# Wider rows for the two "xt" buffers, and another bank ring for the accumulators of the compressed keys and values

## The chip, the cores and the metric

The kernel runs on one core of one Trainium2 chip. The metric is the time of one execution in device microseconds; lower is better. Inputs and outputs are fp32.

## The reference

One layer of a hybrid decoder trunk (DEPTH is 1) on 512 tokens of 1024 features. The input is normalised, multiplied by one wide matrix, and the columns of the product are shared out among four token mixers: A (forgetting attention), B (a gated linear recurrence), C (sparse attention with compressed, selected and windowed keys) and D (chunked spatial gating). Each mixer's output is multiplied by its own SiLU gate and projected; the four are merged by sigmoid gates, projected once more and added to the input.

```python
xn = rms_norm(x, norm_g)
z = xn @ w_in
(qa, ka, va, fa, ga, xb, gb, qc, kcc, vcc, ksc, vsc, kwc, vwc, gate_c, gc,
 ud, vd, gd, mg) = jnp.split(z, split_at, axis=-1)
y_a = fox_attention(rms_norm(qa), rms_norm(ka), va, fa + b_forget)
y_b = rg_lru(xb, ...)
y_c = nsa_attention(rms_norm(qc), kcc, vcc, ksc, vsc, kwc, vwc, sigmoid(gate_c), ...)
y_d = spatial_gating(ud, vd, ...)
ys = stack([y_a * silu(ga), y_b * silu(gb), y_c * silu(gc), y_d * silu(gd)])
proj = einsum('bsnw,nwd->bsnd', ys, w_branch)
merged = sum(sigmoid(mg) * proj, axis=2)
return x + merged @ w_out
```

Inside `nsa_attention` the keys and values of overlapping blocks of 32 positions (stride 16) are compressed by a small network of two layers; the first layer is the part that the change touches:

```python
def compress(t, w1, w2):
    tb = t[:, blk_idx] + cmp_pos[None, None, :, None, :]
    tb = tb.transpose(0, 1, 3, 2, 4).reshape(B, n_cmp, G, CMP_BLOCK * dh)
    return jax.nn.silu(tb @ w1) @ w2
k_c = rms_norm(compress(k_cmp, wk1, wk2), kn_g)
v_c = compress(v_cmp, wv1, wv2)
```

## The kernel before

**Products.** Every fp32 product is made from three matmuls in a reduced fp32 format: both operands are split into a high and a low part, and high times high, high times low and low times high are added up in PSUM. A weight tile of 128 x 1024 (`load`, a 512-KB transfer by SyncE's queue into one of four raw buffers, names `r_...`) is cast to its high part by ScalarE or GpSimd and subtracted by VectorE to its low part (in two halves, names `w_...`). A projected block z is 128 x 512: eight slices of the contraction times three, so 24 matmuls of 512 columns each, in one PSUM bank.

**Stages.** First the input is loaded transposed. `x_norm` needs the row norms, which take time to arrive, so the first three projections (`ka`, `qa`, `va`, with the forget gates `z_gates`) are made from uh and ul, the parts of x times the norm's gain without the row norm; their results are scaled by row afterwards. In the natural layout (`nat`) uh and ul are the stationary operand and the weights move. `z_gates` has the small matrix gw as its stationary operand, and `rps` (the row norms spread over the partitions) the tile `ones`. Behind that all projections use the normed xh and xl. Then come A's attention, the projections and attention of C, laid between the projections of A's gate (`z_ga`), D's gate (`z_gd`), D's u (`z_ud`), C's gate and B; then the merge with its larger weights, which stand in shared sums that transfers with addition prepare in device memory (`dmg...`, `dwb...`), and the output.

**Order.** A planner (class `Order`) takes the instructions as the program emits them, with a cost for each, and writes one order for each of the five engines' queues; a queue is run strictly in that order. Which buffer a tile gets, and so which earlier reader it waits for, also enters the plan. The same emission with another bank can give another order on every queue.

**SBUF places.** Pools lay tiles out by size, one behind another, at the same place of every partition. The pool `xin` holds, in this sequence, the two buffers of the tag "xt" (`head0`/`head1`, later the `xt` tiles of `x_stats`, L415 and L659) and behind them ones, xr, uh, ul, neg, ssa, tsa, rb and gw.

**PSUM banks.** A bank holds 512 fp32 values for each partition. In this stage banks 0 and 1 are a ring of two for scores (`sbank`), 5, 6 and 7 a ring of three for projections (`zbank`). Banks are given out in turn as tiles are asked for. `hidden(nm)` (L1167) runs the first layer of the compression for keys (`hpsk`) and for values (`hpsv`): two halves of w1, and 16 matmuls of 256 columns into one bank, laid between the projections by `yield`. Then ScalarE and VectorE add the parts up (`hsk`, `hsv`), a transpose on TensorE (`tb<-identf,hsv`) and a SiLU follow (`hTv`, `hhv`), and `out` makes the second layer in an s bank (`cok`, `cov`). `sgd` is the reader of a `z_gd` bank: a ScalarE and then a VectorE operation.

Of the kernel before, what the change touches and what calls it, by code (L numbers as in the profile page):

```python
# [11 lines left out]
F32 = mybir.dt.float32  # L12
# [6 lines left out]
P = 128  # L19
S = 512  # L20
D = 1024
KD = D // P
# [41 lines left out]
def f32(ap):  # L64
    return ap.bitcast(F32)
# [260 lines left out]
def tile_hybrid_layer(ctx: ExitStack, tc: tile.TileContext, first, x, xT, units, small, bsp, out):  # L326
    nc = tc.nc
    order = Order(nc)
    ACT, DVE, POOL, PE, DMA = (_Engine(order, e) for e in ("ACT", "DVE", "POOL", "PE", "SP"))

    def pool(name, stack=ctx, **kw):
        return order.pool(stack.enter_context(tc.tile_pool(name=name, bufs=1, reuse_waits="tile", **kw)), stack,
                          kw.get("space"))
# [29 lines left out]
    def zbank(name):  # L363
        return ps_["z"].tile([P, S], F32, tag="z", bufs=ps_["nz"], name=name)
# [9 lines left out]
    def sbank(name):  # L374
        return ps_["s"].tile([P, S], F32, tag="s", bufs=2, name=name)

    def thalf():

        i = ps_["ti"] = (ps_["ti"] + 1) % (2 * len(ps_["tb"]))
        nt = len(ps_["tb"])  # L380
        return ps_["tb"][i % nt][:, 256 * (i // nt):256 * (i // nt) + 256]
# [12 lines left out]
    xin = pool("xin", early)  # L394
# [17 lines left out]
    order.on = True  # L412
    region = ExitStack()
    region.enter_context(tc.manual_schedule())
    head = [xin.tile([P, KD + D], F32, tag="xt", bufs=2, name=f"head{k}") for k in range(2)]  # L415
    for k in range(2):
        DMA.dma_start(head[k], first[:, k])
    maskm = cp.tile([P, S], F32, name="maskm")
    ones = xin.tile([P, P], F32R, name="ones")
    POOL.memset(f32(ones), 1.0)  # L420
# [16 lines left out]
    def hi_cast(dst, src):  # L437
        cnt["hi"] += 1
        if cnt["act"] and cnt["hi"] % cnt["act"] == 0:
            ACT.copy(dst, src)  # L440
        else:
            last["pool"] = POOL.tensor_scalar(dst, src, 1.0, 0.0, op0=ALU.mult, op1=ALU.add)

    def load(key, h):
        raw = wp.tile([P, 1024], F32, tag="raw", bufs=4, name=f"r_{key}{h}")
        DMA.dma_start(raw, units[UIDX[key], :, h * 1024:(h + 1) * 1024])
        return raw
# [149 lines left out]
    def rsqrt(v, y, t):  # L597

        I32 = mybir.dt.int32
        DVE.tensor_scalar(t.bitcast(I32), v.bitcast(I32), 1, None, op0=ALU.logical_shift_right)  # L600
        DVE.tensor_scalar(y.bitcast(I32), t.bitcast(I32), -1.0, float(0x5F3759DF), op0=ALU.mult, op1=ALU.add)
        for _ in range(3):
            DVE.tensor_tensor(t, y, y, op=ALU.mult)
            DVE.scalar_tensor_tensor(t, t, -0.5, v, op0=ALU.mult, op1=ALU.mult)
            DVE.scalar_tensor_tensor(y, t, 1.5, y, op0=ALU.add, op1=ALU.mult)
# [50 lines left out]
    def x_stats():  # L656
        st = cp.tile([P, 3, 4], F32, name="st")
        for t in range(4):
            xt = xin.tile([P, KD + D], F32, tag="xt", bufs=2, name=f"xt{t}")[:, 0:D]  # L659
            DMA.dma_start(xt, x[t * P:(t + 1) * P, :])  # L660
            ACT.activation(xt, xt, AF.Square, accum_out=st[:, 0, t:t + 1])
        DVE.tensor_scalar(st[:, 1, :], st[:, 0, :], 1.0 / D, EPS, op0=ALU.mult, op1=ALU.add)
        rsqrt(st[:, 1, :], rstd[:, 0, :], st[:, 2, :])
        DVE.tensor_tensor(rstd[:, 1, :], rstd[:, 0, :], rstd[:, 0, :], op=ALU.mult)
        DVE.tensor_scalar(rstd[:, 1, :], rstd[:, 1, :], 1.0 / 64, None, op0=ALU.mult)
# [78 lines left out]

    run(nat("ka", uh, ul, emit_z(zk_a, ssa, 0, 8, xin), fetch_first))
    x_stats()
    gq = nat("qa", uh, ul, emit_z(zq_a, ssa, 8, 8, xin))
    run(gq, 10)
# [383 lines left out]
    def mid(name):  # L1132
        return md.tile([P, 2, 1024], F32R, tag="mid", bufs=1, name=name)
# [13 lines left out]
    def compress():  # L1147
# [19 lines left out]
        def hidden(nm):  # L1167
            hps = None
            for h in range(2):
                raw = load("w1" + nm, h)  # L1170
                w = mid(f"w_w1{nm}{h}")
                hi_cast(w[:, 0, :], raw)
                DVE.tensor_tensor(w[:, 1, :], raw, f32(w[:, 0, :]), op=ALU.subtract)
                for _ in range(4):
                    yield 0.0
                if h == 0:
                    hps = zbank("hps" + nm)[:, 0:256]
                for k in range(8):
                    c = 8 * h + k
                    PE.matmul(hps.rearrange("p (j f) -> p j f", j=2), lhsT=ops[nm][:, c].rearrange("p j f -> p (j f)"),  # L1180
                              rhs=w[:, :, k * P:(k + 1) * P], start=c == 0, stop=c == 15)
                    if c < 15:
                        yield 0.15
            hs_ = ap.tile([P, S], F32, tag="ft", bufs=3, name="hs" + nm)
            POOL.memset(hs_[64:128, 0:P], 0.0)
            hs = hs_[0:64, 0:256]
            ACT.copy(hs, hps[64:128, :])
            DVE.tensor_tensor(hs, hps[0:64, :], hs, op=ALU.add)
            DVE.tensor_tensor(hs[:, 0:P], hs[:, 0:P], hs[:, P:2 * P], op=ALU.add)
            yield 0.15  # L1190
            yield 0.15
            hps = thalf()[:, 0:P]
            PE.transpose(hps, hs_[:, 0:P], identf)
            hps = hps[:, 0:64]
            hT = rp2.tile([P, 64], F32, tag="hT", bufs=2, name="hT" + nm)
            hh = rp2.tile([P, 2, 64], F32R, tag="hh", bufs=2, name="hh" + nm)
            ACT.activation(hT, hps, AF.Tanh, scale=0.5)
            DVE.scalar_tensor_tensor(hT, hT, 1.0, hps, op0=ALU.add, op1=ALU.mult)
            ACT.activation(hh[:, 0, :], hT, AF.Identity, scale=0.5)
            DVE.scalar_tensor_tensor(hh[:, 1, :], hT, 0.5, f32(hh[:, 0, :]), op0=ALU.mult, op1=ALU.subtract)  # L1200
            ops[nm] = hh
            yield 0.15
# [13 lines left out]
        for _ in range(4):  # L1216
            yield 0.0
        gk = hidden("k")
        for _ in range(8):
            yield next(gk)  # L1220
        y["c"], ug["t"] = tile8("y_c"), tile8("ug")
        yield from gk
        gv = hidden("v")
        for _ in range(4):
            yield next(gv)
# [781 lines left out]
```

## Time and profile before

| what | value |
|---|---|
| median of 3 runs | 687.35 us (687.24 to 687.45) |
| the profiled execution, its own time | 688.12 us |
| its span (first to last instruction) | 686.4 us |
| granted TensorE clock, mean | 0.999 |
| bytes moved by DMA | 145.45 MB, 212 GB/s |
| VectorE busy | 545.9 us of the span, 80% |
| ScalarE busy | 409.7 us, 60% |
| GpSimd busy | 196.5 us, 29% |

The profile is of one execution: the span is what its rows add up to, and the own time, 1.7 us more, is what that execution took by the measure of the runs. PE is TensorE's matmuls, PEld its loads of stationary operands, DVE is VectorE, ACT ScalarE, POOL GpSimd, SP SyncE. A row of the timeline gives start, length, engine, line, operation, output and inputs, tile sizes, and in brackets how long the engine was idle before and what released it. In a matmul's row the moving operand stands first and the stationary one last. A matmul's record is longer than the distance from one start to the next, because consecutive ones overlap; so a pace is read from starts. Where helpers emit an operation, its line is theirs (L290, L302), and tiles tell rows apart.

### The profile page before, as it was taken

How to read it: one execution, taken by the hardware profiler on the slowest of the kernel's cores; microseconds unless marked ns; L12 is line 12 of the kernel's file. 1: busy time of each engine (PE TensorE's matmuls, PEld its weight loads, DVE VectorE, ACT ScalarE, POOL GpSimd, SP SyncE). 2: the span in 40 equal slices, each digit the busy share in tenths (PEclk: the TensorE clock that was granted, in tenths of full speed). 3: DMA queues.
4: the chain of work that ended last, by engine and by line, in shares of the span. 5: the costliest groups of instructions: out<-in, count | busy, mean ns of one | idle time of the engine just before them, and what ended most of it. 6: DMA issues, size and time to landing. Idle time of an engine off the chain costs nothing.

```text
span 686.4 us, 9750 instructions
## 1 busy us (share of the span) xinstructions
PE 679.4 (99%) x3264; PEld 561.2 (82%) x3264; DVE 545.9 (80%) x1097; ACT 409.7 (60%) x772; POOL 196.5 (29%) x268
## 2 busy tenths in 40 slices
PE   9999999999999999999999999999999999999997
PEld 7888788888888877888887878888888888888886
DVE  6778778788578658889998697957889788848995
ACT  4554458476163247777666895555666666664961
POOL 4111674544346224544351221000202401300000
PEclk9999999999999999999999999999999999999999
DMA  8637076899979998965112224687999999896422
GB/s 322 253 121 245 32 197 211 236 211 262 248 230 302 250 305 214 246 172 106 62 32 71 84 93 169 193 313 241 253 338 300 345 318 368 250 339 207 149 94 93
DMA packets 35010, 145.45 MB, mean 212 GB/s; under 512 B 4096, under 2 KB 7552, under 8 KB 31744
## 3 DMA queue, kind: packets, MB, share of 16 engines
q1 hardware_dynamic: 30064, 108.78, 44.9%
q0 software_dynamic: 4608, 35.65, 24.2%
q8 instruction: 26, 0.43, 0.2%
q10 hardware_dynamic: 288, 0.39, 0.2%
q14 instruction: 24, 0.20, 0.1%
HBM read 139.57 MB, written 58.20 MB: 288 GB/s over the span
## 4 chain that ended last, share of the span: by engine, by line
PE 88%; ACT 4%; DMA 2%; DVE 2%; POOL 1%; issue 1%; DVEq 0%; SPq 0%; POOLq 0%; ACTq 0%
PE tb L290 4%; PE z_ka L290 3%; PE pj L302 3%; PE z_va L290 3%; PE z_qc L290 3%; PE z_qa L290 3%; PE z_xb L290 3%; PE z_ga L290 3%; PE z_vd L290 3%; PE z_gb L302 3%; PE z_kv L290 3%; PE o_s L290 3%; DMA dwb1s<-in_units_dram 2%; PE outy L302 2%; PE mg3y L302 2%; PE mg1y L302 2%
## 5 line engine op out<-in xcount | busy, mean ns | idle before, releaser
L302 POOL TENSOR_SCALAR mark<-mark 128x1 f32<-128x1 f32 x16 | 17.9, 1118 | 104.0 <-ACT mark L302 103.9
L302 DVE TENSOR_TENSOR w_mg<-r_mg,w_mg 128x512 fp32r<-128x512 f32 x48 | 31.8, 687 | 12.7 <-ACT w_mg L302 12.6
L302 PE MATMUL pj<-w_wb,yh 128*128 128x512 f32 x128 | 40.4, 389 | 0.0
L302 ACT CAST w_mg<-r_mg 128x1024 fp32r<-128x1024 f32 x24 | 25.2, 1050 | 11.8 <-issue 6.2
L302 PEld LDWEIGHTS pj<-w_wb,yh 128*128 128x128 f32 x128 | 24.0, 188 | 4.9
L290 POOL TENSOR_SCALAR p_s<-p_s,nm_s 128x512 f32<-128x512 f32 (+3 forms) x32 | 21.3, 681 | 22.4 <-DVE nm_s L290 18.7
L290 POOL TENSOR_SCALAR p_w<-p_w,nm_w 128x128 f32<-128x128 f32 (+3 forms) x32 | 18.4, 589 | 30.6 <-DVE nm_w L290 30.6
L290 ACT ACTIVATE p_s<-p_s,nm_s 128x512 f32<-128x512 f32 (+3 forms) x32 | 17.9, 561 | 13.7 <-DVE nm_s L290 13.2
L290 POOL TENSOR_SCALAR p_a<-p_a,nm_a 128x128 f32<-128x128 f32 (+3 forms) x32 | 20.9, 666 | 16.8 <-DVE nm_a L290 16.7
L290 ACT ACTIVATE p_w<-p_w,nm_w 128x256 f32<-128x256 f32 (+3 forms) x32 | 17.9, 561 | 12.5 <-DVE nm_w L290 12.4
L302 PE MATMUL pj<-w_wb,yl 128*128 128x512 f32 x64 | 25.2, 394 | 0.1
L290 PE MATMUL z_xb<-xh,w_xb 128*128 128x512 f32 x64 | 24.6, 410 | 0.0
L290 ACT CAST ph_a<-tb 128x512 fp32r<-128x512 f32 (+1 forms) x24 | 12.4, 517 | 18.8 <-PE tb L290 18.5
L290 PE MATMUL z_ud<-xh,w_ud 128*128 128x512 f32 x64 | 23.5, 405 | 0.0
L290 PE MATMUL z_gd<-xh,w_gd 128*128 128x512 f32 x64 | 22.5, 396 | 0.3 <-DVE sgd L290 0.3
L290 PE MATMUL z_ga<-xh,w_ga 128*128 128x512 f32 x64 | 21.9, 396 | 0.0
L302 PE MATMUL z_gb<-xh,w_gb 128*128 128x512 f32 x64 | 21.1, 396 | 0.0
L302 DVE TENSOR_TENSOR w_wb<-r_wb,w_wb 128x512 fp32r<-128x512 f32 x28 | 19.4, 717 | 1.4 <-POOL w_wb L302 0.9
L290 ACT ACTIVATE p_a<-p_a,nm_a 128x512 f32<-128x512 f32 (+3 forms) x32 | 17.8, 560 | 3.0 <-DVE nm_a L290 2.9
L290 DVE CUSTOM_DVE_ANT_0 p_a<-s_a,maskm 128x512 f32<-128x512 f32 (+3 forms) x32 | 15.0, 488 | 4.6 <-PE tb L290 2.8
L302 POOL TENSOR_SCALAR w_wb<-r_wb 128x1024 fp32r<-128x1024 f32 x8 | 10.8, 1350 | 26.9 <-PE pj L302 7.7
L290 ACT CAST ph_s<-tb 128x512 fp32r<-128x512 f32 (+1 forms) x24 | 12.2, 511 | 9.0 <-PE tb L290 8.5
(750 smaller groups left out, 2382.3 us busy)
## 6 DMA issues: line engine op xcount, KB each, us to landing
r_mg<-in_units_dram SPq DMA_DIRECT2D x16, 512.0 KB, 7.1
r_wb<-in_units_dram SPq DMA_DIRECT2D x12, 512.0 KB, 3.7
dmg<-in_units_dram POOLq DMA_DIRECT2D x4, 1024.0 KB, 9.9
r_mg<-dmg SPq DMA_DIRECT2D x8, 512.0 KB, 7.9
dmg0s<-in_units_dram POOLq DMA_DIRECT2D x3, 1024.0 KB, 10.4
dmg2s<-in_units_dram POOLq DMA_DIRECT2D x3, 1024.0 KB, 13.1
dmg1s<-in_units_dram POOLq DMA_DIRECT2D x3, 1024.0 KB, 11.3
r_mg0s<-dmg0s SPq DMA_DIRECT2D x6, 512.0 KB, 4.7
```

The costliest lines, as they stand in the source:

```text
L290: getattr(self.eng[name], method)(*args, **kw)
L302: return lambda *args, **kw: real(*args, **kw).ins
```

## The change

Two edits. The tiles of tag "xt" get rows of D + 32 = 1056 floats instead of D + KD = 1032, of which the transfers and operations use the same 1032 and 1024 as before. And the accumulators of the compression's first layer are asked for from the s ring instead of the z ring.

```diff
-    head = [xin.tile([P, KD + D], F32, tag="xt", bufs=2, name=f"head{k}") for k in range(2)]
+    head = [xin.tile([P, D + 32], F32, tag="xt", bufs=2, name=f"head{k}") for k in range(2)]
     for k in range(2):
-        DMA.dma_start(head[k], first[:, k])
+        DMA.dma_start(head[k][:, 0:D + KD], first[:, k])
...
         for t in range(4):
-            xt = xin.tile([P, KD + D], F32, tag="xt", bufs=2, name=f"xt{t}")[:, 0:D]
+            xt = xin.tile([P, D + 32], F32, tag="xt", bufs=2, name=f"xt{t}")[:, 0:D]
...
                 if h == 0:
-                    hps = zbank("hps" + nm)[:, 0:256]
+                    hps = sbank("hps" + nm)[:, 0:256]
```

In the built program the first "xt" buffer stays at byte 89344 of its partition and the second moves from 93472 to 93568. Behind them ones moves from 97600 to 97792, xr from 98112 to 98304, uh from 114496 to 114688, ul from 130880 to 131072, neg from 147264 to 147456, rb from 164416 to 164608 and gw from 166464 to 166656. xh (7424), xl (23808) and the three weight buffers (40192, 48384 and 56576) stay.

The PSUM banks before: hpsk and hpsv both in 6, z_gd_1996 and z_gd_2001 (the first two z_gd tiles) both in 7. After: hpsk and hpsv in 0, cok and cov in 1, and the z_gd tiles in 5, 6, 7, 5. The orders of the engines agree up to the first hpsk matmul, differ from there up to the end of the z_xb projections, and agree again behind them.

TensorE at the end of hpsk. `z_gd_1996` and `z_gd_2001` are the first two z_gd tiles, `z_gd_2012` the third, `tb_...` are transposes. Before:

```order
L290 MATMUL hpsk<-w_w1k_1994,tblk 128x256
L290 MATMUL tb_81<-identf,p_s_1970 128x128 x2
L290 MATMUL tb_81<-identf,p_s_1974 128x128
L290 MATMUL tb_1936<-identf,p_s_1974 128x128 x2
L290 MATMUL z_gd_2012<-xh,w_gd_2003 128x512
L290 MATMUL z_gd_2012<-xl,w_gd_2003 128x512
L290 MATMUL z_gd_2001<-xh,w_gd_1998 128x512
```

After:

```order
L290 MATMUL z_gd_1996<-xh,w_gd_1992 128x512
L290 MATMUL hpsk<-w_w1k_1994,tblk 128x256
L290 MATMUL z_gd_2001<-xh,w_gd_1998 128x512
L290 MATMUL z_gd_2001<-xl,w_gd_1998 128x512
L290 MATMUL z_gd_2001<-xh,w_gd_1998 128x512 x2
```

The five transposes of scores and two matmuls of the third tile no longer stand there, and z_gd_2001, now in a bank of its own, follows z_gd_1996 at once.

VectorE where the sums of hpsv are made; `w_ud_2032` is the low part of a z_ud weight tile. Before:

```order
L290 SCALAR_TENSOR_TENSOR sgd<-sgd,z_gd_2017 128x512
L290 TENSOR_TENSOR hsv<-hpsv,hsv 64x256
L290 TENSOR_TENSOR w_ud_2032<-r_ud_2031,w_ud_2032 128x512
L290 TENSOR_TENSOR hsv<-hsv 64x128
L290 SCALAR_TENSOR_TENSOR kc_1946<-tb_1936,cc,kc_1946 64x32
```

After:

```order
L290 SCALAR_TENSOR_TENSOR sgd<-sgd,z_gd_2017 128x512
L290 TENSOR_TENSOR w_ud_2032<-r_ud_2031,w_ud_2032 128x512 x2
L290 TENSOR_TENSOR hsv<-hpsv,hsv 64x256
L290 TENSOR_TENSOR hsv<-hsv 64x128
L290 SCALAR_TENSOR_TENSOR hTv<-hTv,tb_81 128x64
```

Both halves of the split now stand ahead of both additions.

GpSimd at the same place; the cast to `w_ud_2032` is what the split waits for, and `dwb1s_197` is a transfer with addition that waits for an earlier one. Before:

```order
L290 DMA dwb3s_202<-in_units_dram 128x1024
L290 TENSOR_SCALAR w_w1v_2016<-r_w1v_2015 128x1024
L290 DMA dwb1s_197<-in_units_dram 128x1024
L290 TENSOR_SCALAR w_ud_2032<-r_ud_2031 128x1024
L290 TENSOR_SCALAR w_ud_2052<-r_ud_2051 128x1024
```

After:

```order
L290 TENSOR_SCALAR w_w1v_2016<-r_w1v_2015 128x1024
L290 DMA dwb3s_202<-in_units_dram 128x1024
L290 TENSOR_SCALAR w_ud_2032<-r_ud_2031 128x1024
L290 DMA dwb1s_197<-in_units_dram 128x1024
L290 TENSOR_SCALAR w_ud_2052<-r_ud_2051 128x1024
```

The cast now stands ahead of the issue of dwb1s_197, and behind that of dwb3s_202, which before stood ahead of the w_w1v cast.

## The prediction

> **What bounds the kernel now.** I read the head of the page first, then the waits of TensorE, then its pace stage by stage. PE is the engine's record of matmuls, PEld that of its loads of the stationary operand.
>
> ```profile
> span 686.4 us, 9750 instructions
> PE 679.4 (99%) x3264; PEld 561.2 (82%) x3264; DVE 545.9 (80%) x1097; ACT 409.7 (60%) x772; POOL 196.5 (29%) x268
> PE 88%; ACT 4%; DMA 2%; DVE 2%; POOL 1%; issue 1%; DVEq 0%; SPq 0%; POOLq 0%; ACTq 0%
> ```
>
> PE is busy 679.4 of 686.4 us, and the chain that ended last is PE for 88%. What all waits of PE cost is small:
>
> ```profile
> engine line waited for: us in total, times, longest us
> PE warm L302 <- DVE warm L302: 1.5, 1, 1.5
> PE tb L290 <- POOL p_w L290: 0.5, 1, 0.5
> PE tb L290 <- DVE hsv L290: 0.4, 1, 0.4
> PE z_gd L290 <- DVE sgd L290: 0.3, 1, 0.3
> PE tb L290 <- DVE pl_a L290: 0.2, 1, 0.2
> ```
>
> So the time moves only if PE's own pace moves, or one of these waits. (PE's order is fixed when the program is built, so a wait isn't filled.) "Busy" hides the pace: two stretches that are both 40.00 of 40 us busy hold different numbers of matmuls.
>
> ```profile
> core 0: us, PE busy (x) PEld busy (x) DVE busy (x) ACT busy (x) POOL busy (x), PEclk, DMA share, GB/s
> 6.93:71.56 64.63, 64.63 (x278) 51.80 (x277) 51.65 (x104) 31.38 (x58) 12.69 (x12) 1.00 0.62 223
> 10.00:50.00 40.00, 40.00 (x173) 32.08 (x172) 31.00 (x59) 21.80 (x40) 8.66 (x8) 1.00 0.62 231
> 140.00:160.00 20.00, 20.00 (x112) 17.09 (x111) 18.96 (x51) 14.91 (x35) 8.22 (x13) 1.00 1.08 286
> 460.00:500.00 40.00, 40.00 (x178) 33.14 (x177) 30.92 (x50) 24.17 (x36) 4.74 (x9) 1.00 0.88 271
> ```
>
> Both 40-us stretches hold 128x512 matmuls alone, at a granted clock of 1.00. The exact pace comes from starts, 24 matmuls apart (a weight tile's 8 times 3):
>
> ```profile
> 28.39 0.39 PE L290 MATMUL z_qa<-w_qa.00_166,uh 128*128 128x512 f32 x1
> 33.99 0.39 PE L290 MATMUL z_qa<-w_qa.01_172,uh 128*128 128x512 f32 x1
> 461.32 5.60 PE L302 MATMUL mg0y<-w_mg0s,xs 128*128 128x512 f32 x24
> 466.76 0.39 PE L302 MATMUL mg0x<-w_mg,xh 128*128 128x512 f32 x1
> ```
>
> 33.99 − 28.39 = 5.60 us, 233.3 ns each; 466.76 − 461.32 = 5.44 us, 226.7 ns each. The early stage pays 6.67 ns more for the same shape, and the records say so too:
>
> ```profile
> L290 PE MATMUL z_qa<-w_qa.00_166,uh x16: 394/394/394, 28.4 to 33.8; 128*128 128x512 f32 x16
> L290 PE MATMUL z_gates<-xh,gw x8: 394/394/394, 51.3 to 60.1; 128*128 128x512 f32 x8
> L290 PE MATMUL rps<-dh,ones x1: 394/394/394, 39.4 to 39.4; 128*128 128x512 f32 x1
> L302 PE MATMUL mg0x<-w_mg,xh x32: 389/389/389, 450.4 to 472.0; 128*128 128x512 f32 x32
> ```
>
> The slow ones use uh, ul, gw or ones as the stationary operand (the last name of a row). z_gates has another moving operand, xh, and another output layout, and is as slow; so what all of them share is the place of the stationary tile. In the built program uh, ul, gw and ones begin 64 B off a multiple of 128 B in their partition; xh, xl and the weight tiles begin on one. One 512-B row of such a stationary tile touches five 128-B pieces instead of four.
>
> **The change part by part.**
>
> *Padding.* It removes and adds no instruction. A row of the two "xt" buffers grows by 96 B, so with two buffers everything allocated behind them moves by 192 B: uh from 114496 to 114688, ul from 130880 to 131072, gw from 166464 to 166656, ones from 97600 to 97792, all now on a multiple of 128 B. The second buffer moves by 96 B, onto one as well. The sum: 277 starts between the first and last row of the 6.93 to 71.56 stretch (64.63 / 277 = 233.3 ns). If all run at 226.7, 277 × 6.67 ns = 1.85 us; the 29 others of that stage (306 in all: 96 each of z_ka, z_qa, z_va, 16 z_gates, 2 rps) run at the start or between short transposes, and I leave them out. With them the ceiling is 306 × 6.67 = 2.04 us. Floor 0, if the address isn't the cause. A loss I exclude for this part: no instruction is longer and no transfer has more bytes. I take 1.85, nearest to the row, because nothing waits there that could eat it: PE is 64.63 of 64.63 us busy, while DVE has 13 us of slack and DMA runs at a share of 0.62. Should the weight tiles come too late at the quicker pace, PE would wait on a w_va split next; those splits follow buffers that PE itself frees, and so move with it.
>
> The Trainium skill ("TensorE: Matmul & The Clock Gate", section "Back-to-back issue gap") gives a warm gap of N/2.4 + 2.5 ns for an isolated matmul, about 216 ns for 512 columns, and a measured sustained one of about 131 ns; neither has a term for where an operand lies. Both paces above are longer, and they differ at the same N and the same clock, so the trace doesn't agree with a gap set by N alone. By that rule the padding would be worth 0, and the sum would be the bank part's alone.
>
> *Banks.* hpsk and hpsv (accumulators of the products with w1k and w1v, each filled by 16 short matmuls laid far apart between others) leave the ring of three z banks for that of two s banks. Before, with one z bank held, consecutive z_gd tiles meet in one bank:
>
> ```profile
> 222.06 0.40 PE L290 MATMUL z_gd<-xl,w_gd 128*128 128x512 f32 x1
> 222.79 0.50 PE L290 MATMUL z_gd<-xh,w_gd 128*128 128x512 f32 x1 [0.34 <-DVE sgd L290]
> 223.13 0.39 PE L290 MATMUL z_gd<-xl,w_gd 128*128 128x512 f32 x1
> 222.05 0.69 DVE L290 SCALAR_TENSOR_TENSOR sgd<-sgd,z_gd 128x512 f32<-128x512 f32 x1 [2.20 <-ACT sgd L290]
> ```
>
> The next tile had to wait for sgd, its predecessor's reader, to end at 222.74. Start to start the pair takes 0.73 + 0.34 = 1.07 us instead of 2 × 0.227 = 0.45: 0.61 us. After the change z_gd goes through banks 5, 6, 7, 5, with two tiles between users of a bank, so this wait goes. I take −0.6; between 0 (another wait in its place) and −0.6.
>
> What hpsk meets instead: the s bank must be read by the custom DVE operation on the last score tile before its first matmul. DVE's order now has that operation ahead of the trs sum and the w_gd split. The row of the first hpsk matmul:
>
> ```profile
> 206.28 0.28 PE L290 MATMUL hpsk<-w_w1k,tblk 128*128 128x256 f32 x1
> 204.81 0.69 DVE L290 TENSOR_TENSOR w_ga<-r_ga,w_ga 128x512 fp32r<-128x512 f32 x1
> ```
>
> Behind the w_ga half, free for the next at about 205.4, come two such operations on 256 columns (0.4 each by the spacing of DVE's rows), so the bank is free near 206.3; PE arrives one matmul later than before, at 206.5. Cost 0, at most 0.2. The score stage itself had ended, so nothing else asks for s banks until cok (same ring) and sc.
>
> *The wait that stays.* hsv, the transposed sum of hpsv, is the other stall here:
>
> ```profile
> 245.91 0.39 PE L290 MATMUL z_ud<-xh,w_ud 128*128 128x512 f32 x1
> 246.74 0.33 PE L290 MATMUL tb<-identf,hsv 128*128 128x128 f32 x1 [0.44 <-DVE hsv L290]
> 245.80 0.69 DVE L290 TENSOR_TENSOR w_ud<-r_ud,w_ud 128x512 fp32r<-128x512 f32 x1 [3.08 <-POOL w_ud L290]
> 246.41 0.28 DVE L290 TENSOR_TENSOR hsv<-hsv 64x128 f32<-64x128 f32 x1
> 243.87 0.81 POOL L290 DMA_DIRECT2D dwb1s<-in_units_dram  x1 [9.17 <-DMA dwb1s<-in_units_dram]
> 244.44 1.33 POOL L290 TENSOR_SCALAR w_ud<-r_ud 128x1024 fp32r<-128x1024 f32 x1
> ```
>
> The transpose started 0.83 behind its predecessor, 0.60 late. DVE stood 3.08 us on POOL's cast of w_ud, and POOL stood 9.17 us on a transfer (dwb1s) whose issue was ahead of the cast. Now the cast stands ahead of that issue, which makes it earlier; but DVE has both halves of the w_ud split ahead of both hsv operations. PE comes to the transpose sooner: it was due at 246.14 (245.91 + 0.23); five matmuls of 512 columns (1.13) and five short transposes (about 0.1 each) fewer stand ahead of it, and the sgd wait (0.61) is gone, which gives about 244.0, with every clock still that of before. The cast then waits for its own r_ud:
>
> ```profile
> r_ud<-in_units_dram SPq DMA_DIRECT2D x4, 512.0 KB, 11.5
> ...
> DMA to landing us min/median/max: 4.8/11.5/15.7
> ...
> 224.54 1.57 SPq L290 DMA_DIRECT2D r_ud<-in_units_dram  x2
> ```
>
> The second of that pair, issued near 225.8 (the pair ends at 226.11, an issue takes 0.33), would land at about 237.3 by the median of 11.5, at 241.5 by the longest, 15.7; I take the longest for it. From 241.5: the cast 1.33, two halves 0.6 each by the spacing of the rows, and the two hsv operations (0.28 for the shown one, some 0.4 for the wider) give 244.7: a wait of 0.7 instead of 0.6. Were it to land by 240.8, the wait would be gone, −0.6. I take 0, near the first, since the trace has no sooner landing of this load. Ahead of the cast POOL now issues dwb3s, whose first copy SP issues about when it issues that r_ud; I expect it down no later. On SP's queue the second w1v load now goes ahead of the dmg1s copy and one r_ud ahead of dwb3s; POOL's p_s products and its weight casts are regrouped. No row of before shows their cover in the new order, so I allow ±0.5 for all of them together: the size of the largest single wait in the list above but for the start's.
>
> **The sum.** −1.85 − 0.6 + 0 = −2.45. Against the profiled run: 686.4 − 2.45 = 683.95 of span, 688.12 − 2.45 = 685.67 of its own time, which lies 0.77 above the median. Against the median, 687.35 − 2.45 = 684.9.
>
> **The rivals.**
>
> A, the sum above: 684.9; own range 684.0 to 685.7 (ceiling 2.04 and a vanished hsv wait at one end, the ±0.5 and a kept wait at the other).
>
> B, the padding does nothing: the pace belongs to the stage (its DMA writes, or the products' natural layout) and not to the address. For it: uh, gw and ones are used in that stage alone, so no row shows one of them elsewhere. Against it: z_gates and rps share neither the moving operand nor the output with z_qa and yet have the same 394 ns, and the stretch at 460 us is fast at a higher DMA share (0.88 against 0.62). Then only −0.6 is left: 686.7, no measurable change. The Trainium skill's "SBUF — State Buffer", section "Door 1: The DMA port swizzle (why [64,N] ≈ [32,N])", speaks of cachelines of 16 bytes in SBUF; an offset of 64 B is whole such lines, so by that page an extra piece wouldn't exist and B would hold. The row of 394 against 389 ns doesn't settle it.
>
> C, the 1.85 us are won by 77 us and given back: from 140 us on the transfers are dense (share 1.08 in the row above), and a stage that runs at their pace would start earlier but end at the same time. Against it: PE has no wait of any length on a DMA in the list. I price it at a loss of 1 to 1.85, 685.9 to 686.7.
>
> D, slower: the hsv transpose waits long. All of DVE's hsv work now stands behind a cast that stands on r_ud. It decides when that landing slips far enough: the 2.45 saved and 1.37 of margin must be used up on top of the present 0.6: a wait of 4.4 us, so a landing at about 245.2 instead of 241.5, 19.4 us after its issue. The row of r_ud has 15.7 as its longest; 3.7 us more was seen for none of the four. Its time would be 688.8 or more.
>
> **How the numbers follow.** A measurement of this kernel can tell about 0.2% from no change, 1.37 us: faster is below 685.98, slower above 688.72. Chances: A 0.70, B 0.15, C 0.09, D 0.06. A is all faster; C falls about half on each side; B counts as no change, with a share of runs pushed below by lucky waits (0.03). That gives faster 0.77, same 0.17, slower 0.06. The range runs from A's lower end to B's price with a bit of the ±0.5 cut away: 683.8 to 686.8 leaves out D, part of C and B above it, and little below.
>
> **What would show it.** Padding right: rows of z_qa, z_gates and rps at 389 ns; 24 matmuls from z_qa.00 to z_qa.01 in 5.44; about 178 matmuls from 10 to 50 us; z_kv's first start at about 76.9 instead of
>
> ```profile
> 78.74 0.48 PE L290 MATMUL z_kv<-w_kv.00_792,xh 128*128 128x512 f32 x1
> ```
>
> With 394 and 78.7 there, B holds. Banks right: no wait of z_gd on sgd near 222 us. C shows as a first start of hpsk still near 206.3. D shows as a tb wait on hsv of several us, with POOL's cast released by r_ud. The forecast is wrong if the early pace stays, or if a new wait above 1 us shows up between 206 and 370 us, where the orders differ.

## The result and the profile after

The changed kernel takes 691.58 us (4 runs, 690.9 to 692.37) against 687.4 before; the ratio is 1.0057, with a 95% interval of 1.0044 to 1.0071. It is slower by 4.2 us, where 2.45 less was forecast. The profiled execution after has a span of 690.7 us and an own time of 692.37.

The head of the page, and the waits of PE:

```profile
span 690.7 us, 9747 instructions
...
PE 87%; DVE 7%; DMA 2%; ACT 1%; POOL 1%; issue 1%; DVEq 0%; POOLq 0%; ACTq 0%
```

```profile
engine line waited for: us in total, times, longest us
PE cok L290 <- ACT hhk L290: 2.6, 1, 2.6
PE warm L302 <- DVE warm L302: 1.5, 1, 1.5
PE tb L290 <- POOL p_s L290: 0.8, 3, 0.4
PE tb L290 <- DVE pl_a L290: 0.2, 1, 0.2
```

The waits on sgd and on hsv are gone. A new one of 2.6 us, on ACT's hhk, stands at the head.

The padding did what was forecast. The row of z_qa among those of tile uh (min, median and max ns of one):

```profile
L290 PE MATMUL z_qa<-w_qa.00_166,uh x16: 389/389/389, 27.6 to 32.8; 128*128 128x512 f32 x16
```

The first starts of z_qa.00 and z_qa.01 in the timeline, 5.44 us apart:

```profile
27.60 0.39 PE L290 MATMUL z_qa<-w_qa.00_166,uh 128*128 128x512 f32 x1
...
33.04 0.39 PE L290 MATMUL z_qa<-w_qa.01_172,uh 128*128 128x512 f32 x1
```

The stretch from 10 to 50 us, in the columns shown before:

```profile
10.00:50.00 40.00, 40.00 (x178) 33.11 (x177) 32.16 (x60) 22.85 (x43) 8.80 (x8) 1.00 0.62 231
```

And the first z_kv in the timeline:

```profile
76.89 0.47 PE L290 MATMUL z_kv<-w_kv.00_792,xh 128*128 128x512 f32 x1
```

389 ns instead of 394, 178 matmuls instead of 173, and z_kv at 76.89 instead of 78.74: 1.85 us. The lead was still 1.79 at the first z_gd. It was lost behind 220 us. The chain there, from the timelines of POOL, SP, ACT and PE:

```profile
211.81 0.81 POOL L290 DMA_DIRECT2D dwb1s<-in_units_dram  x1
212.84 0.50 SPq L290 DMA_DIRECT2D dmg1s<-in_units_dram  x1
214.59 0.33 SPq L290 DMA_DIRECT2D r_gd<-in_units_dram  x1
225.73 1.04 ACT L290 CAST w_gd<-r_gd 128x1024 fp32r<-128x1024 f32 x1 [4.71 <-DMA r_gd<-in_units_dram]
226.68 0.22 ACT L290 ACTIVATE hTk<-tb 128x64 f32<-128x64 f32 x1
227.18 0.26 ACT L290 ACTIVATE hhk<-hTk 128x64 fp32r<-128x64 f32 x1 [0.29 <-DVE hTk L290]
224.53 0.39 PE L290 MATMUL z_gd<-xh,w_gd 128*128 128x512 f32 x1
227.49 0.77 PE L290 MATMUL cok<-w2k,hhk 128*64 128x64 f32 x2 [2.58 <-ACT hhk L290]
```

The load r_gd, issued at 214.59, takes 11.1 us to land. ACT has its cast ahead of hTk and hhk, so these two wait for it, though they need nothing of it; cok needs hhk, and PE stands idle for 2.58 us. Before that idle stretch ends, TensorE's clock is halved. Stretches of the changed kernel (the column behind POOL's is the granted clock):

```profile
223.54:226.96 3.42, 1.37 (x6) 0.77 (x5) 0.03 (x1) 1.17 (x2) 0.84 (x1) 1.00 1.01 308
226.96:233.78 6.82, 6.15 (x18) 5.05 (x19) 5.16 (x20) 1.26 (x5) 1.04 (x1) 0.50 0.98 223
234.00:236.00 2.00, 2.00 (x11) 1.68 (x11) 0.00 (x0) 0.00 (x0) 0.00 (x0) 1.00 0.91 291
```

The clock is 0.50 for 6.8 us; in the 6.15 of them that PE is busy, half the speed costs about 3.1. "Busy" says nothing of this: the stretch is 6.15 of 6.82 us busy, with 18 matmuls.

Before, the same cast stood at the same place in ACT's order, but the load had landed. The timelines of ACT, POOL and SP before:

```profile
222.91 1.05 ACT L290 CAST w_gd<-r_gd 128x1024 fp32r<-128x1024 f32 x1 [0.50 <-POOL w_w1v L290]
220.94 0.82 POOL L290 DMA_DIRECT2D dwb1s<-in_units_dram  x1 [0.38 <-issue]
208.92 1.41 SPq L290 DMA_DIRECT2D dmg1s<-in_units_dram  x1
216.53 0.33 SPq L290 DMA_DIRECT2D r_gd<-in_units_dram  x1
```

Its r_gd took at most 6.4 us (216.53 to 222.91). The dwb1s addition was issued behind it, at 220.94, where it now is issued at 211.81; and the dmg1s copy 7.6 us ahead of it, where now it is 1.75.

### The profile page after: what moved, and what is told of

The parts are those of the page before. It is cut to its first block, busy times and chain, and to the rows that moved or that the text cites. A ratio compares the mean times of both kernels' runs of the same rounds, so it can differ in the third digit from the quotient of the medians.

```text
span 690.7 us, 9747 instructions
## 1 busy us (share of the span) xinstructions
PE 681.1 (99%) x3264; PEld 563.1 (82%) x3264; DVE 546.6 (79%) x1097; ACT 409.0 (59%) x772; POOL 195.5 (28%) x268
## 4 chain that ended last, share of the span: by engine, by line
PE 87%; DVE 7%; DMA 2%; ACT 1%; POOL 1%; issue 1%; DVEq 0%; POOLq 0%; ACTq 0%
PE pj L302 6%; PE tb L290 3%; PE z_qc L290 3%; PE z_va L290 3%; PE z_ka L290 3%; PE z_vd L290 3%; PE z_gb L302 3%; PE z_qa L290 3%; PE z_ud L290 3%; PE z_kv L290 3%; PE mg3y L302 2%; PE outy L302 2%; PE mg1y L302 2%; PE mg2y L302 2%; PE mg0y L302 2%; PE o_s L290 2%
## 5 line engine op out<-in xcount | busy, mean ns | idle before, releaser
L290 POOL TENSOR_SCALAR p_s<-p_s,nm_s 128x128 f32<-128x128 f32 (+3 forms) x32 | 19.5, 629 | 23.0 <-ACT p_w L290 6.9
L290 PE MATMUL z_gd<-xh,w_gd 128*128 128x512 f32 x64 | 24.3, 418 | 0.0
L302 POOL TENSOR_SCALAR w_wb<-r_wb 128x1024 fp32r<-128x1024 f32 x8 | 11.1, 1387 | 29.9 <-PE pj L302 15.3
```

What stands on the lines that cost most here:

```text
L290: getattr(self.eng[name], method)(*args, **kw)
L302: return lambda *args, **kw: real(*args, **kw).ins
```

## The experiments

Medians are set against runs of before on the same chip (687.45 to 687.48).

**The padding alone.** The diff without its last line; the order on every engine is that of before.

> Only the wider rows of the two xt buffers; the accumulators stay in the z ring, and the order on every engine is that of before. Theory (the pace follows the place of the stationary tile, and the loss of the change comes from the bank part alone): z_qa's records at 389 ns, z_kv's first start near 76.9 us, and the gain kept to the end, 687.4 - 1.85 = 685.5 us; no wait of PE above 1 us behind the start, granted clock 1.00 throughout. Rival (the earlier PE also upsets the transfers of the dense stage, whatever the order): part or all of the 1.85 us is lost again between 140 and 260 us, 686.5 us or more.

686.18 us, ratio 0.9981 (0.9972 to 0.9989). The padding is a gain by itself, 1.3 us in the median; the pace in the records is 226.7 ns from 8.4 us to the end of z_va, and no wait of PE above 0.5 us but the start's. In its profiled run z_kv started only 1.08 sooner: between 5.6 and 8.2 us its first matmuls stood 0.43 us apart, the half-clock pace, for longer than in the trace of before. That stretch at the start differs from run to run (0.3 to 1.3 us above the steady pace in six traces), whatever the padding.

**The banks alone.**

```diff
-                    hps = zbank("hps" + nm)[:, 0:256]
+                    hps = sbank("hps" + nm)[:, 0:256]
```

> Only the accumulators' move to the s ring; rows of before, the order on every engine is that of the changed kernel. Theory (the order of the bank part makes the load r_gd land late, ACT's cast blocks the chain to cok, PE idles 2.6 us and its clock is halved behind that): PE waits 2 to 3 us for ACT's hhk near 227 us, a granted clock of 0.5 for 6 to 7 us behind it, 691.6 + 1.85 = 693.4 us. Rival (it takes both parts together: the early PE of the padding brings the transfers on top of each other): no such wait, 687.4 - 0.6 = 686.8 us.

690.23 us, ratio 1.0046 (1.0033 to 1.006): slower, but less than expected. The profiled run (689.63, the fastest of six) has a clock of 1.00, and a small wait in the list of PE's waits:

```profile
PE cok L290 <- ACT hhk L290: 0.5, 1, 0.5
...
PE cok L290 <- DVE hhk L290: 0.2, 1, 0.2
```

Here PE comes to cok 1.6 us later, but r_gd is issued 1.6 later too (216.21 instead of 214.59). The load took 9.0 us (cast from 225.25), against 11.1 in the changed kernel's trace. The padding's lead alone doesn't make that difference: in two traces with padding and the new order that follow below (the cast behind hhk, work in the idle stretch) r_gd took 9.1 us. So the profiled run of the changed kernel has the longest landing seen with this order.

In the medians the changed kernel is nevertheless 1.3 slower than this one. All four of its runs have a low mean clock (0.995 to 0.998), here one of six has (0.997, the slowest, 692.93). Why the padding, a gain by itself, makes the loss at cok larger isn't shown.

**The cast behind hhk.** In the changed kernel two instructions are moved, on ACT's and DVE's queues.

```diff
 ACT:
-  CAST w_gd_2014<-r_gd_2013
   ACTIVATE hTk
   ACTIVATE hhk
+  CAST w_gd_2014<-r_gd_2013
 DVE:
-  TENSOR_TENSOR w_gd_2014 (first half)
   SCALAR_TENSOR_TENSOR hhk
+  TENSOR_TENSOR w_gd_2014 (first half)
```

> The changed kernel with two instructions moved: ACT's cast of the fourth w_gd tile stands behind the hTk and hhk operations instead of ahead of them, and DVE's first half of its split behind hhk's low part. Nothing else moves. Theory (the late load costs time only because its cast stands ahead of the chain to cok on ACT's queue): r_gd still lands near 225.6, the wait of cok goes, the clock stays at 1.00; 691.6 - 2.6 (wait) - 3.1 (half clock) = 685.9 us. Rival (the split of w_gd becomes the next late thing): PE waits for DVE's w_gd at z_gd_2017 by 1 us or more, and the time stays above 687 us.

687.32 us, ratio 0.9998 (0.999 to 1.0007); 4.3 us less than the changed kernel. All waits of PE in its trace:

```profile
PE warm L311 <- DVE warm L311: 1.5, 1, 1.5
PE tb L299 <- POOL p_s L299: 0.9, 3, 0.4
```

The wait of cok is gone, no wait for w_gd came in its place, and the clock is 1.00. In this trace r_gd landed sooner than expected (cast from 223.99, not 225.6), but hTk and hhk were through before it (hhk began at 223.48). So this one cast ahead of the chain makes the loss against before. It isn't the whole distance to the forecast: 687.3 is 1.4 above the 685.9 of the theory, and 1.1 above the padding alone.

**The addition cut down.**

```diff
+ if first dwb1s addition: args = [a[:, 0:64] for a in args]
```

> The changed kernel, same order, with one transfer cut down: POOL's first addition into the dwb1s sum in device memory moves 64 of 1024 columns (the rest of that sum is left out). Theory (crowding: that addition now starts 9 us sooner and shares the DMA engines with the dmg1s copy and the r_gd load): r_gd lands by about 223 instead of 225.65, the wait of cok falls below 0.5 us, the clock stays, about 686 us. Rival (the queue: r_gd stands behind the 1-MB dmg1s copy on SP's queue and would be late without the addition too): r_gd lands at 224.5 or later, cok waits 1.5 us or more, 689 us or more.

687.05 us, ratio 0.9995 (0.9986 to 1.0004). ACT's timeline:

```profile
221.72 1.05 ACT L293 CAST w_gd<-r_gd 128x1024 fp32r<-128x1024 f32 x1
222.97 0.23 ACT L293 ACTIVATE hTk<-tb 128x64 f32<-128x64 f32 x1 [0.20 <-PE tb L293]
```

The kernel leaves out the other 960 columns of that addition. With the order unchanged, r_gd, issued at 215.15, took at most 6.6 us, and nothing waits for it; with the whole addition it took 9.0 to 11.1 in five traces of this order. So the addition makes the load late, and not the place behind the dmg1s copy on SP's queue, which is the same in this kernel. Whether it takes the copy beside the addition wasn't tried.

**Work in the idle stretch.**

```diff
+ 12 x matmul(cok's bank, lhsT=xh[:, 0, 0:128], rhs=xh[:, 0, :])
  matmul(cok, ...)
```

> The changed kernel with 12 idle matmuls of 512 columns (12 x 0.227 = 2.7 us of work that nothing uses) put into TensorE's order right ahead of cok, where it waited 2.6 us. Nothing else moves. Theory (half of the loss is TensorE's clock, halved behind the idle stretch): cok still starts where ACT's hhk lets it, at about 227.5, but the granted clock stays at 1.00 behind it; 691.6 - 3.1 = 688.5 us. Rival (the low clock has another cause, such as the load of the whole chip at that point): the clock is 0.5 behind cok as before, and the time 691.6 us or more.

689.6 us, ratio 1.0031 (1.0018 to 1.0043): 2.0 less than the changed kernel, 2.3 more than with the cast moved. The clock:

```profile
225.00:230.00 5.00, 5.00 (x27) 4.16 (x26) 3.09 (x10) 1.26 (x5) 1.05 (x1) 1.00 1.02 270
...
230.00:235.00 5.00, 5.00 (x26) 4.17 (x25) 2.93 (x12) 0.00 (x0) 1.27 (x2) 1.00 0.98 280
```

The clock stays at 1.00 (0.999 to 1.000 in all six runs), so the idle stretch is what halves it, and not the load of the chip at that point. cok starts at 227.46, as in the changed kernel, but here it isn't hhk that holds it. ACT's rows:

```profile
223.60 1.05 ACT L295 CAST w_gd<-r_gd 128x1024 fp32r<-128x1024 f32 x1 [2.62 <-DMA r_gd<-in_units_dram]
...
225.06 0.26 ACT L295 ACTIVATE hhk<-hTk 128x64 fp32r<-128x64 f32 x1 [0.28 <-DVE hTk L295]
```

In this run r_gd landed 2.1 us sooner than in the changed kernel's trace, and cok stands behind the twelve matmuls themselves (224.73 to 227.46). So the run prices twelve matmuls at 2.3 us. That they last about as long as the wait in the changed kernel's trace (2.7 and 2.58) makes an estimate: of the 4.3 us about 2.3 are the wait and 2.0 the clock, in the median. For the clock 3.1 were expected from the one profiled run, whose mean of 0.995 is the lowest of its four (0.997 and twice 0.998 in the others).

**The banks, with the cast moved.** The two edits together, no padding.

> The banks alone (no padding) with the two moved instructions of the third experiment, so that cok doesn't wait for the cast. It shows what the new order is worth without the wait and the clock. Theory (the waits on sgd and hsv that it removes, 0.6 each, are paid back by later transposes that wait for POOL's p_s products, some 1.5 us): 687.45 + 0.3 = 687.8 us, within 0.3 of before up to 688.6 (what the padded pair of runs gives: 687.3 - 686.2 = 1.1 more). Rival (the order is a gain once the cast is out of the way): 686.8 us or less.

688.74 us, ratio 1.0017 (1.0008 to 1.0026). So even without the wait the new order costs 1.3 us, though the sgd and hsv waits are gone. Its waits:

```profile
PE tb L299 <- POOL p_s L299: 0.7, 2, 0.4
PE pj L311 <- DVE yl L311: 0.6, 2, 0.5
PE tb L299 <- DVE pl_a L299: 0.2, 1, 0.2
```

Measured from start to start against the usual pace of each shape, two steps before transposes of p_s are too long, by 0.61 (at 322 us in this trace) and 0.46 (340 us), in all the kernels with this order and in none with the order of before. Why POOL's products come late for them I didn't try to undo. But they don't locate the 1.3 us. PE's orders differ up to the first pj products, a little beyond the z_xb projections, and there the trace of before (368.72) and this one (368.69) stand level: by then the waits that are gone have been paid back, and no more. The profiled run of before was itself some 0.7 above the medians of before. So the 1.3 is a difference of medians whose place isn't shown.

**Four matmuls ahead of the stall.** The padding alone, the order of before, and four z_gd_2012 matmuls moved ahead of z_gd_2001, to fill the wait on sgd.

> The padding alone, with the order of before but for four matmuls of the third z_gd tile that now stand ahead of the second tile's first, so that TensorE has work while DVE reads sgd. Theory (the stall of sgd, 0.6 us, can be filled without a new bank): no wait of z_gd for sgd, 686.2 - 0.6 = 685.6 us. Rival (the stall was cover for something later): another wait of PE in its place, 686.2 us.

685.89 us, ratio 0.9976 (0.9967 to 0.9985): the fastest of all, but not clearly below the padding alone. The wait on sgd is gone; in the profiled run another has grown, as the rival said:

```profile
PE tb L299 <- DVE hsv L299: 0.8, 1, 0.8
PE tb L299 <- POOL p_w L299: 0.8, 2, 0.5
```

**Where the stationary tile lies.** Three kernels, one run each, to test my reading of the pace (five pieces of 128 B instead of four).

```diff
- xt rows: [P, D + 8]         + [P, D + 16]     (all behind moves by 64 B)
- xt rows: [P, D + 8]         + [P, D + 24]     (by 128 B)
- ones: [P, P]                + [P, P + 8]      (uh, ul, gw by 32 B)
```

> Before, with rows of D + 16 instead of D + 8 in the two xt buffers and no change of banks: uh at 114560, ul, gw and ones with it, on a multiple of 128 B but not of 256. Theory (a stationary tile off a multiple of 128 B costs 6.7 ns a matmul): 389 ns records and 226.7 ns from start to start in z_qa, as with D + 32. Rival (it takes a multiple of 256 or 512 B): 394 ns and 233.3.

> Before, with rows of D + 24, no change of banks: everything behind moves by 128 B, so uh, ul, gw and ones stay 64 B off a multiple of 128; the second xt buffer moves by 64 B. Theory: 394 ns and 233.3 ns stay, z_kv's first start near 78.7. Rival (the wider rows themselves, or the place of the second xt buffer, make the stage faster): 389 ns.

> Before, with 8 unused floats behind the tile ones: uh, ul and gw move by 32 B to 96 B off a multiple of 128; ones stays 64 B off. No change of banks. Theory (any offset from a multiple of 128 B makes a 512-B row touch five pieces of 128 B): 394 ns and 233.3 as before. Rival (only the offset of 64 B is slow, or 96 is slower still): z_qa at 389 ns, or above 394.

The first starts of z_qa.00 and z_qa.01 in the timelines; first rows of D + 16:

```profile
28.36 0.39 PE L290 MATMUL z_qa<-w_qa.00_166,uh 128*128 128x512 f32 x1
33.93 0.40 PE L290 MATMUL z_qa<-w_qa.01_172,uh 128*128 128x512 f32 x1
```

Rows of D + 24:

```profile
28.31 0.39 PE L290 MATMUL z_qa<-w_qa.00_166,uh 128*128 128x512 f32 x1
33.81 0.39 PE L290 MATMUL z_qa<-w_qa.01_172,uh 128*128 128x512 f32 x1
```

The longer ones tile:

```profile
28.21 0.39 PE L290 MATMUL z_qa<-w_qa.00_166,uh 128*128 128x512 f32 x1
33.83 0.39 PE L290 MATMUL z_qa<-w_qa.01_172,uh 128*128 128x512 f32 x1
```

5.57, 5.50 and 5.62 us for 24 matmuls. My reading falls: with uh on a multiple of 128 B (D + 16) the stage is hardly faster than before (5.60), and 64 B off one (D + 24) it is faster by two thirds of the way to 5.44. The times were 686.86, 687.1 and 687.01, which tells nothing apart.

**Everything moved by 64 B.** These numbers fit a period of 256 B, but uh's place had always been varied against weights at a fixed place. The unused tile `fit` is left out, so that uh, xh and the weight buffers all move down by 64 B; what was 64 B behind a multiple of 256 now lies on one. Not every tile moves: yh, the high part of a mixer's output in the merge, stays at 163584, a multiple of 256, in both programs.

```diff
-    cp.tile([P, 16], F32, name="fit")
+    pass
```

> Before, without an unused tile of 64 B in the first pool, so that every tile behind it moves down by 64 B: uh, ul, gw, ones from 64 to 0 past a multiple of 256 B, and xh, xl and the weight buffers from 0 to 192 past one. The order is that of before. Theory (the stationary tile's own place modulo 256 B sets the pace: 226.7 ns at 0, 233.3 at 64, 234.2 at 96, 232.1 at 128, 228.8 at 192): z_qa at 226.7, and the blocks with xh or a weight as the stationary operand (mg, z_ga) at about 228.8. Rival (the place of the stationary tile relative to the moving one counts, which stays 64 B in z_qa and 0 in mg): z_qa at 233.3, mg at 226.7.

z_qa's starts in the timeline:

```profile
28.71 0.39 PE L290 MATMUL z_qa<-w_qa.00_165,uh 128*128 128x512 f32 x1
34.31 0.39 PE L290 MATMUL z_qa<-w_qa.01_171,uh 128*128 128x512 f32 x1
```

By tile, the pj products of the merge (stationary yh) in the kernel before, with the weights on a multiple of 256 B:

```profile
L302 PE MATMUL pj<-w_wb,yh x128: 388/389/398, 368.7 to 423.7; 128*128 128x512 f32 x128
```

The same in this kernel, with the weights 192 past one, and mg0x (both operands 192 past one):

```profile
L302 PE MATMUL pj<-w_wb,yh x128: 392/394/398, 367.8 to 423.3; 128*128 128x512 f32 x128
...
L302 PE MATMUL mg0x<-w_mg,xh x32: 388/389/389, 450.1 to 471.7; 128*128 128x512 f32 x32
```

The rival holds. z_qa stays at 5.60 with uh on a multiple of 256 B; pj, 389 ns before, now has 394, though its stationary tile hasn't moved, only the moving one; mg0x stays fast off a multiple of 256. What counts is where the stationary tile lies relative to the moving one. By that difference, modulo 256 B:

| stationary minus moving | from start to start, z_qa | kernel |
|---|---|---|
| 0 | 226.7 ns | changed kernel |
| 64 | 233.3 | before, and the last one |
| 96 | 234.2 | ones + 8 |
| 128 | 232.1 | D + 16 |
| 192 | 229.2 | D + 24 |

The rows are rounded to 0.01 us, which is 0.4 ns of a matmul here. The last kernel's time was 689.72, one run. The Trainium skill ("TensorE: Matmul & The Clock Gate", section "Step-by-step: what each phase is for") gives TensorE two independent read ports for the two operands; by that their relative place shouldn't matter, and here the runs differ from it by up to 7.5 ns a matmul. What in the memory causes it is open.

**How long TensorE may idle.** The padding alone, and at four places of the merge small ACT copies (7, 5, 4 and 14) between blocks.

> The kernel with the padding alone, and in the merge stage at four places a chain of 7, 5, 4 and 14 small ACT copies between one block's last matmul and a small matmul that waits for them (some 1.3 to 3.5 us of idle TensorE each; the trace gives the lengths). Seen so far: an idle stretch of 0.85 us left the granted clock at 1.00, one of 2.6 us was followed by 6.6 us at 0.50. Theory (the clock falls when TensorE has been idle for longer than a bound between 0.85 and 2.6 us): the stretches below the bound show a clock of 1.00 behind them, those above it 0.50 for 6 to 7 us. Rival (it takes a longer idle time, and the fall in the changed kernel had help from the stretch ahead of it): only the longest, or none, is followed by a low clock.

The small matmuls that should have waited didn't: the program placed the copies elsewhere. But the copies delayed ACT's casts there, which made four idle stretches all the same: three of 1.69 us and one of 2.31 us. The time was 696.87 us, one run. One stretch of each kind in the timeline of PE:

```profile
453.59 0.39 PE L302 MATMUL mg0x<-w_mg,xh 128*128 128x512 f32 x1
455.67 0.96 PE L302 MATMUL mg0y<-w_mg0s,xs 128*128 128x512 f32 x3 [1.69 <-ACT w_mg0s L302]
...
496.48 1.24 PE L302 MATMUL mg2y<-w_mg2s,xs 128*128 128x512 f32 x3 [2.31 <-ACT w_mg2s L302]
```

Stretches of 3.41 us around them, first one with 1.69 us of idling, then that of 2.31 and the one behind it:

```profile
452.62:456.03 3.41, 1.72 (x8) 1.09 (x8) 1.68 (x3) 2.62 (x8) 0.00 (x0) 1.00 1.01 401
...
493.58:496.99 3.41, 1.10 (x5) 0.63 (x4) 2.11 (x4) 2.72 (x8) 0.00 (x0) 1.00 1.07 253
496.99:500.40 3.41, 3.41 (x10) 2.46 (x10) 2.06 (x4) 1.25 (x3) 0.00 (x0) 0.50 1.33 471
```

Behind 1.69 us the clock stays at 1.00, three times out of three; behind 2.31 it is 0.50 for 3.41 us, as around 2.58 in the changed kernel for 6.82. The lengths weren't set by me, and one stretch of 2.31 is a single case. (The 0.85 us named above are from start to start, 226.17 to 227.02 in the trace of the banks alone; idle was 0.46 of it. Between 0.5 and 1.69 us the traces have one idle stretch behind the start, 0.83 in the kernel with four matmuls moved, and its clock stayed too.)

The length alone isn't the rule, though. In every trace here the recorded clock changes only a whole number of times 3.413 us after its first rise: the fall in the changed kernel 65 times (5.09 to 226.96), the one here 144 times (5.47 to 496.99). In the last such piece of 3.41 us ahead of the fall PE was busy for 1.37 us there and for 1.10 here; in the pieces around the 1.69-us stretches it was busy for 1.72, 1.72 and 1.80, and the clock stayed. So these traces put the border between 40% and 50% of such a piece. By that a stretch of 2.3 us that is cut in two by the end of a piece need not lower the clock; no run shows that case. The Trainium skill ("TensorE: Matmul & The Clock Gate", section "What's actually happening") has the clock halved after an idle window of about 3.4 us; here 2.3 and 2.6 us of idling were enough. Its window does agree with how long the clock stayed low, one and two of them, and with the 3.413 us.

## Why the prediction was wrong, point by point

- *Padding, −1.85.* The size was right: 1.85 us at z_kv, and −1.3 us in the median of the padding alone, whose interval (−1.9 to −0.8) holds it. The reason was not. "One 512-B row touches five pieces instead of four" speaks of the stationary tile's own place; the runs show its place relative to the moving operand. In before, with the weights on a multiple of 256 B, the two readings can't be told apart, and I took the one for shown. Rival B, that the address does nothing, falls, and with it a gap set by N alone.
- *Banks, −0.6.* The wait on sgd did go. But the order that came with it costs 1.3 us in the median even with the cast moved, and no wait at the place I followed by hand shows it; where it is lost stays open.
- *The wait that stays, 0.* hsv's wait, 0.6, went as well; nothing hung on its r_ud. I had followed this one chain because it waited before, and made rival D of it.
- *"So I allow ±0.5 for all of them together."* This is the step that failed. Under it lay the moves on SP's and POOL's queues, the first dwb1s addition among them, which I didn't name. They put the landing of r_gd off from 222.91 or sooner to 225.73, on an ACT queue that had 0.6 us of slack: before, the cast began at 222.91, held by POOL and not by the load, and hTk stood 0.6 us for PE behind it. The cast ahead of hhk costs +4.3 (the changed kernel against the one with the cast moved), by estimate +2.3 for the wait and +2.0 for the clock. With the padding's −1.3 and the −0.6 taken as won, the term is some +6.1 where 0 ± 0.5 was allowed. The bound came from the largest wait in the list of before, and such a list shows nothing of a load that comes just in time. The prediction's own sign of being wrong, a new wait above 1 us between 206 and 370 us, is what came: 2.6 us at 227.
- *Rival D, slower.* It gave "slower" 0.06 and 688.8 us or more, but by a wait on hsv; that wait went. The slowdown isn't a point for D's mechanism.
- *A wait costs its length.* Each wait in the sum, rival D's too, was priced at its own length. The wait of 2.58 us cost TensorE's clock as well, which here nearly doubles it.
- *A's own range.* From the terms named there its ends come out at 684.1 and 685.4, not 684.0 and 685.7; nothing hangs on it.
- *The sum of medians.* −1.3 (padding alone) + 1.3 (new order without the wait) + 4.3 (the cast ahead of hhk) = +4.3; measured +4.2.

## What to carry to other kernels

Where a change reorders queues, follow every load that is cast between the changed places: its issue, its neighbours on the DMA engines, its landing against the cast, and what stands behind that cast on its engine though it needs nothing of it. A list of waits shows only what was late, and the next loss comes from what was just in time. A wait of TensorE of about 2 us or more should be priced with the clock behind it: the waits here that left TensorE busy for 40% or less of a piece of 3.41 us halved it. And where two stages run the same shape at different paces at the same clock, vary the places of both operands before naming the cause.

## What the runs showed of the hardware

- A 128x512 matmul's pace depends on where its stationary operand lies relative to the moving one in SBUF, modulo 256 B as far as five differences show: 226.7 ns at 0, up to 234.2 at 96.
- Idle stretches of TensorE of 1.69 us left the clock alone; with 2.31 and 2.58 us came 3.4 and 6.8 us at half of it. The clock changed only at whole multiples of 3.413 us after its first rise.
- A 512-KB load took 9.0 to 11.1 us beside an addition in device memory and a 1-MB copy, in five traces; with the addition cut to a sixteenth it took at most 6.6.
